# Other distances between the operands of a product in SBUF, one block of products moved ahead in the cross-attention, and four idle products fewer

## The chip, the cores and the metric

The kernel runs on one NeuronCore of a Trainium2 chip. Its time is the device time of one launch in microseconds, taken as the median of several runs. A profile is one execution recorded by the hardware profiler; its times count from the first instruction.

## The reference

One layer of a bidirectional encoder over 512 tokens of 1024 features, in float32. Two mixers (a state-space scan and a gated MLP in chunks) are merged and added to the residual; then comes cross-attention to 256 memory tokens with four heads, then a SwiGLU block. What the change touches is the second half:

```python
def memory_cross_attention(hn, memn, w_q, w_k, w_v, w_o):
    q = (hn @ w_q).reshape(bsz, seq, XATTN_HEADS, XATTN_HEAD_DIM)
    k = (memn @ w_k).reshape(bsz, MEM_LEN, XATTN_HEADS, XATTN_HEAD_DIM)
    v = (memn @ w_v).reshape(bsz, MEM_LEN, XATTN_HEADS, XATTN_HEAD_DIM)
    s = jnp.einsum('blhd,bmhd->bhlm', q, k) * (XATTN_HEAD_DIM ** -0.5)
    p = jax.nn.softmax(s, axis=-1)
    o = jnp.einsum('bhlm,bmhd->blhd', p, v).reshape(bsz, seq, D_MODEL)
    return o @ w_o

def swiglu(hn, w_gate, w_up, w_down):
    return (jax.nn.silu(hn @ w_gate) * (hn @ w_up)) @ w_down

def reference(x, mem, ...):
    ...
    h = h + merged @ w_out[i]
    h = h + memory_cross_attention(rms_norm(h, xattn_norm_g[i]), rms_norm(mem, mem_norm_g), ...)
    h = h + swiglu(rms_norm(h, ffn_norm_g[i]), w_gate[i], w_up[i], w_down[i])
    return rms_norm(h, final_norm_g)
```

## The kernel before

**Products in three parts.** Every float32 operand is split into a rounded half and the rest, `hi` and `lo`: `split` (L85, L86) copies on ScalarE (ACT) into a float32r tile and subtracts on VectorE (DVE). Every product then is three products on TensorE (PE), hi x hi, hi x lo and lo x hi, all added in PSUM (`mm3` at L350, `product` at L1273). A product has a stationary operand of 128 columns, loaded by its own instruction (PEld in the profile, done while the product before it streams), and a moving operand of 256 or 512 columns.

**Weights.** A list, `plan`, holds all blocks of weights in the order of use. `next_w` hands out the next block, starts the loads of those that follow (SP's queue) and splits the ones two ahead into three rotating pairs of tiles, `whi` and `wlo`.

**Which operand moves.** In `feat` and in `product` the weights are stationary and the tokens move; in `tokm` the tokens are stationary and the weights move. The cross-attention's keys use `feat` with the memory's tokens `mn` (products of 256 columns, rows pf<-mn), its values `tokm` with the same tokens (512 columns, rows pt<-whi,mn), the queries `product` with the tokens `hn` (rows qx, qv, qq), and gate and up `product` with the tokens `fn` (rows px, pv, pq; one block of each goes through L350, rows pf<-fn). Queries, gate, up and down are computed by Strassen's scheme with seven products in place of eight, on halves of the tokens and of the features; sums of tokens lie in extra tiles (`hsd`, `hse`, `s1`, `s2`, `s4`).

**Where operands lie.** A tile starts at a fixed byte of each partition. The weights' six tiles start at bytes 30,016 to 50,496, all equal modulo 512; the slot that holds first `xn`, then `hn`, then `fn` starts at 70,976, which is the same modulo 512. The kernel lays the halves of the tokens off that start: `APART = (48, 112)` are floats, so `hi` begins 192 and `lo` 448 bytes (modulo 512) from the weights; both are 192 modulo 256, and this is called the distance below. `hn`, `fn`, the keys' `mn` and the token sums of queries, gate and up all have it. `xn`, `w_out`'s, `w_xo`'s and the down block's operands have distance 0. In the values of the memory, where the weights move, they stand at 64 modulo 256 from the tokens.

**The attention.** For each head `scores` makes the products (rows psc), takes the row maxima (L1236), exponentials on ACT (L1239) and scales the probabilities on DVE (L1243); `turn` transposes them on TensorE (rows ppt) and splits them into `p_hi` and `p_lo`; `values` multiplies by the memory's values (rows po, two of six products a head, each in a PSUM bank) and splits the result into `ot`. `w_xo`, the output product, is a `tokm`: it takes four PSUM banks of the five in the pool (rows pt), and goes through four blocks of weights; block 0 needs the values of head 0, block 1 those of head 1, blocks 2 and 3 those of heads 2 and 3. Its last two blocks are held and done token tile by token tile, and a `hook` is called before them, which makes the values of heads 2 and 3. `later(n, f)` and `tick` put work off by so many slots while the program is written; the framework orders each engine's instructions by priority in the order in which they are written and by its own estimate of when each can start, except where `in_order` pins them.

**The start.** `idles(n)` puts n products of a tile of ones on TensorE, pinned in order: ten at the head (each is two rows in the profile), two more in `first_rows` behind the two products (rows pg) that spread the norm's gain `g_row` over the partitions. `first_rows` then scales the first 128 tokens (L563) with that gain and the factor `r`, transposes them (rows ptr) and goes on to the first block of weights.

Of the kernel before, what the change touches and what calls it, by code (L numbers as in the profile page):

```python
# [20 lines left out]
NT = T // P  # L21
KD = D // P
# [30 lines left out]
def hybrid_layer_kernel(  # L53
# [11 lines left out]
    w_q, w_k, w_v, w_xo = w_q[0], w_k[0], w_v[0], w_xo[0]  # L65
# [11 lines left out]
    def bank(name):  # L77
        return pm.tile([P, 512], F32, tag="mm", name=name)

    def aux(name, shape=(P, 512)):  # L80
        return pa.tile(list(shape), F32, tag="aux", name=name)
# [30 lines left out]
        return hi, lo  # L112


    APART = (48, 112)

    def halves_at(t, k, n, off):

        return tuple(t[:, i * k * n + o:(i + 1) * k * n + o].rearrange("p (k n) -> p k n", k=k)
                     for i, o in enumerate(off))  # L120
# [3 lines left out]
    def sums_place(i, k, n, off=(0, 0)):  # L124
        return halves_at(sums_pool[0].tile([P, 2 * k * n + 128], F32R, tag=f"s{i}", name=f"s{i}", bufs=1), k, n, off)
# [196 lines left out]
    def next_w(*key):  # L322
        i = used_w[0]
        used_w[0] += 1
        assert len(plan[i][0]) == len(key) and plan[i][0][1:] == key[1:] and plan[i][0][0] is key[0]
        for j in range(i, min(i + FAR + 1, len(plan))):
            begin(j, i)
            if j - 1 >= len(tiles) and j - 1 <= i + SPLITS:
                split_w(j - 1)
        for j in range(len(tiles), min(i + SPLITS + 1, len(plan))):  # L330
            split_w(j)
        tile_, tiles[i] = tiles[i], None
        return tile_
# [52 lines left out]

    RATE = 0.8

    def tokm(w, c0, act, nk, evac, ntok=NT, last=2, kpt=2, hook=None, cut=None, t0=0):

        toks = range(t0, t0 + ntok)
        ps = {t: bank(f"pt{t - t0}") for t in toks}
        nw = nk // kpt
        held = []
        full = slice(0, 512)
        for wi in range(nw):
            hi, lo = next_w(w, wi * kpt, kpt, c0, 512)
            held.append((wi, hi, lo))
            if hook is not None and wi == nw - last:
                hook()  # L400
            if wi < nw - last:
                todo, held = held, []
                for t in toks:
                    end = cut is not None and t == ntok - 1 and wi == nw - last - 1
                    tok_block(ps[t], t, todo, act, kpt, full, wi == 0, end)
                    if end:
                        cut(None, ps[t])
                tick(1.3 * ntok)
        for t in toks:
            if cut is not None and t == ntok - 1:  # L410
                for i in range(2):
                    p = aux("pcut", (P, 256))
                    tok_block(p, t, held, act, kpt, slice(256 * i, 256 * i + 256), True, True)
                    cut(i, p)
            else:
                tok_block(ps[t], t, held, act, kpt, full, nw == last, True)
                evac(t, ps[t])
            tick(1.3 * len(held))

    def tok_block(ps, t, ws, act, kpt, cs, first, final):  # L420
        tsl = slice(t * P, (t + 1) * P)
        for i, (wi, hi, lo) in enumerate(ws):
            for k in range(kpt):
                kk = wi * kpt + k
                mm3(ps, (act[0](kk, tsl), act[1](kk, tsl)) if callable(act[0]) else
                    (act[0][:, kk, tsl], act[1][:, kk, tsl]),
                    (hi[:, k, cs], lo[:, k, cs]), first and i == k == 0,
                    final and i == len(ws) - 1 and k == kpt - 1)
# [3 lines left out]
    def later(n, fn):  # L432

        side["later"].append((side["now"] + n, fn))
# [23 lines left out]
    def gain(src, name):  # L458
        t = np_.tile([P, D], F32, tag="gain", name=name, bufs=2)
        nc.sync.dma_start(t, src.partition_broadcast(P))  # L460
        return t
# [60 lines left out]
    def token_slot(name, off=(0, 0)):  # L522

        return halves_at(sp.tile([P, 2 * KD * T + 128], F32R, tag="B", name=name), KD, T, off)
# [8 lines left out]
    def idles(n):  # L533
        for i in range(n):
            in_order(nc.tensor.matmul(idle, ones, ones, start=True, stop=True))

    idles(10)
    warm = np_.tile([P, 1], F32, tag="ms", name="warm", bufs=2)
    nc.scalar.activation(warm, mhalf, AF.Square)

# [577 lines left out]
    for t in range(NT):  # L1118
        nc.sync.dma_start(h[:, t, :], x[t * P:(t + 1) * P, :])
    hn_hi, hn_lo = token_slot("hn", APART)  # L1120

    def mq_tile(name, off):
        return ap_.tile([P, KD * M + 64], F32R, tag="mq", name=name, bufs=2)[:, off:off + KD * M]

    mn_hi, mn_lo = (mq_tile(nm, APART[0]).rearrange("p (k t) -> p k t", k=KD) for nm in ("mn_hi", "mn_lo"))
    g_mem = gain(mem_norm_g, "g_mem")

    def mem_norm(t):
# [8 lines left out]
    for t in range(NM):  # L1137
        later(0.2 + t, lambda t=t: mem_norm(t))
    shift = ap_.tile([P, APART[0]], F32, name="shift")
    nc.gpsimd.memset(shift, 0.0)  # L1140
# [6 lines left out]
    def add_evac(half, layer, fin, fin0=None):  # L1147

        def f(t, ps):
            nc.vector.tensor_tensor(h[:, t, HALF[half]], h[:, t, HALF[half]], ps, ALU.add)  # L1150
            sum_sq(hss[:, layer, t, half:half + 1], h[:, t, HALF[half]])
            if half == 1:
                fin(t, hss[:, layer, t, :])
            elif fin0 is not None:
                fin0(t)
        return f
# [36 lines left out]
    part_at = lambda t, i: t[:, i:i + 1024].rearrange("p (k n) -> p k n", k=4)  # L1193
    hops[6], hops[5] = halves_at(sd, 4, 256, APART), halves_at(se, 4, 256, APART)
    hops[3] = (part_at(sd, 2176 + APART[0]), part_at(se, 2048 + APART[1]))

# [25 lines left out]
    def scores(hd):  # L1222
        q_hi, q_lo = qs.pop(hd)
        scale = XD ** -0.5
        prob = ap_.tile([P, NT, M], F32, tag="prob", name="prob", bufs=1) if hd % 2 == 0 else \
            np_.tile([P, NT, M], F32, tag="gain", name="prob", bufs=2)
        for i in range(2):
            ps = bank("psc").rearrange("p (t m) -> p t m", t=2)
            for tt in range(2):
                t = 2 * i + tt  # L1230
                tsl = slice(t * P, (t + 1) * P)
                for k in range(2):
                    mm3(ps[:, tt, :], (q_hi[:, k, tsl], q_lo[:, k, tsl]),
                        (kt_hi[:, 2 * hd + k, :], kt_lo[:, 2 * hd + k, :]), k == 0, k == 1)
            mx, nm, sm, rs = (ap_.tile([P, 2], F32, tag=k, name=k, bufs=4) for k in ("mx", "nm", "sm", "rs"))
            nc.vector.tensor_reduce(mx, ps, AX.X, ALU.max)  # L1236
            nc.vector.tensor_scalar(nm, mx, -scale, None, ALU.mult)
            for tt in range(2):
                nc.scalar.activation(prob[:, 2 * i + tt, :], ps[:, tt, :], AF.Exp, bias=nm[:, tt:tt + 1],  # L1239
                                     scale=scale, accum_out=sm[:, tt:tt + 1])  # L1240
            nc.vector.reciprocal(rs, sm)
            for tt in range(2):
                nc.vector.tensor_scalar(prob[:, 2 * i + tt, :], prob[:, 2 * i + tt, :], rs[:, tt:tt + 1], None, ALU.mult)  # L1243
        return prob
# [11 lines left out]
    def values(hd, p_hi, p_lo):  # L1256
        for dt_ in range(2):
            ps = bank("po")
            cs = slice(hd * XD + dt_ * P, hd * XD + dt_ * P + P)
            for mt in range(NM):  # L1260
                mm3(ps, (vts[0][:, mt, cs], vts[1][:, mt, cs]), (p_hi[:, mt, :], p_lo[:, mt, :]), mt == 0, mt == NM - 1)
            split(ot_hi[:, 2 * hd + dt_, :], ot_lo[:, 2 * hd + dt_, :], ps)
# [35 lines left out]
    pts = {}  # L1298

    def turn(hd, probs):  # L1300
        pts[hd] = turn_probs(hd, probs)
# [39 lines left out]
    ot_lo = slot("E", (P, KD, T), F32R, "ot_lo")  # L1341
    values(0, *pts.pop(0))
    probs2 = scores(2)
    turn(1, probs1)
    probs3 = scores(3)
    values(1, *pts.pop(1))
    turn(2, probs2)
    later(1, lambda: turn(3, probs3))

    g_f = gain(ffn_norm_g[0], "g_f")  # L1350
    ot = (ot_hi, ot_lo)
    fn_hi, fn_lo = token_slot("fn", APART)
    fn = (fn_hi, fn_lo)

    tokm(w_xo, 0, ot, KD, add_evac(0, 1, None), hook=lambda: [values(i, *pts.pop(i)) for i in (2, 3)])
    at.close()
    ff = ExitStack()
    fp = ff.enter_context(tc.tile_pool(name="ffn", bufs=1))
# [46 lines left out]
    a11, a12, a21, a22 = full[:, K0, T0], full[:, K1, T0], full[:, K0, T1], full[:, K1, T1]  # L1405

    def make_op(q, i, src):
        ops[q] = sums_place(i, 4, 256, APART)
        split(*ops[q], src)

    def sum1():
# [13 lines left out]
    ops = {1: fn_q(K0, T0), 2: fn_q(K1, T0), 7: fn_q(K0, T1), 4: fn_q(K1, T1)}  # L1425
# [86 lines left out]
    for i, u in enumerate(UNITS):  # L1512
        final = i == len(UNITS) - 1
        x, v = begun
        q = unit_bank("pq")
# [122 lines left out]
    for i in range(2):  # L1638
        p = aux("pcut", (P, 256))
# [37 lines left out]
```

## Time and profile before

| what | value |
|---|---|
| median of 3 runs (lowest to highest) | 914.19 us (914.08 to 915.07) |
| the profiled execution | 917.2 us, span of the instructions 915.4 us |
| TensorE products, weight loads | 98% and 87% of the span |
| VectorE, ScalarE, GpSimd | 68%, 52%, 11% |
| DMA | 153.80 MB, mean 168 GB/s |
| keys | about 418 to 443 us |
| values of the memory | about 443 to 466 us |
| queries, scores | about 466 to 519 us |
| probabilities, values, `w_xo` | about 519 to 578 us |
| gate and up | about 578 to 810 us |
| down | from about 792 us to the end |

In rows of groups, "out<-in" names the tile written and those read, then come the operand sizes and the count, and behind the bar the busy time, the mean ns of one and the idle time before. Products overlap in the pipeline, so the ns of one is longer than the step from one to the next. Idle time is put down to the work that ended last.

### The profile page before, as it was taken

Reading aid. Unit: us, or ns where it says so; the run is one execution under the profiler, and the core shown is the slowest. Engines: PE = TensorE matmul, PEld = TensorE weight load, DVE = VectorE, ACT = ScalarE, POOL = GpSimd, SP = SyncE. Lnnn points to the kernel's source line nnn. Section 1 sums busy time; section 2 is a strip of 40 time slices with the busy share of each in tenths; the row PEclk is TensorE's granted clock in tenths of the full one; section 3 lists DMA queues with packets and bytes.
Section 4 is the critical chain, followed back from the end, with each engine's and each line's share of the span. In section 5 each row is a group of like instructions: output and inputs, shape, how many; then the busy total and the mean of one; then the engine's idle time right before and its main releaser. Section 6 shows DMA issues by size and latency. Waiting matters only on the chain.

```text
span 915.4 us, 14510 instructions
## 1 busy us (share of the span) xinstructions
PE 900.7 (98%) x5650; PEld 796.5 (87%) x5650; DVE 623.8 (68%) x1018; ACT 475.4 (52%) x696; POOL 102.1 (11%) x161
## 2 busy tenths in 40 slices
PE   9999999999999999999999999999999999999996
PEld 6888888888888887789899878999999999988885
DVE  5696662888753236858956836776778767899875
ACT  5542985144364334447655634745455454655664
POOL 1004420110025200101000001100020100000000
PEclk9999999999999999999999999999999999999999
DMA  8456574685546577863578416526788873246672
GB/s 252 148 148 185 124 181 141 174 193 149 153 134 146 127 219 206 275 198 120 175 216 252 139 47 184 161 88 149 189 202 212 221 186 93 69 138 200 191 244 90
DMA packets 111974, 153.80 MB, mean 168 GB/s; under 512 B 13521, under 2 KB 78561, under 8 KB 111842
## 3 DMA queue, kind: packets, MB, share of 16 engines
q1 hardware_dynamic: 93026, 128.27, 44.1%
q0 software_dynamic: 16288, 23.57, 15.9%
q10 hardware_dynamic: 2592, 1.05, 0.5%
q8 instruction: 44, 0.72, 0.3%
q14 instruction: 24, 0.20, 0.1%
HBM read 146.08 MB, written 38.24 MB: 201 GB/s over the span
## 4 chain that ended last, share of the span: by engine, by line
PE 90%; ACT 4%; DVE 3%; issue 1%; POOL 0%; DMA 0%; POOLq 0%; SPq 0%; DVEq 0%; ACTq 0%
PE pf L350 27%; PE pt L350 16%; PE px L1273 12%; PE pq L1273 6%; PE dx L350 6%; PE dq L350 3%; PE pv L1273 3%; PE qx L1273 2%; PE dv L350 2%; PE pk L786 2%; PE ptr L506 1%; PE qq L1273 1%; DVE wlo L86 1%; PE po L350 1%; ACT whi L85 1%
## 5 line engine op out<-in xcount | busy, mean ns | idle before, releaser
L86 DVE TENSOR_TENSOR wlo<-wraw,whi 128x1024 fp32r<-128x1024 f32 (+1 forms) x139 | 164.9, 1187 | 109.5 <-ACT whi L85 107.8
L85 ACT CAST whi<-wraw 128x1024 fp32r<-128x1024 f32 (+1 forms) x139 | 142.2, 1024 | 163.0 <-PE pf L350 67.0
L350 PE MATMUL pf<-xn,whi 128*128 128x512 f32 x448 | 140.1, 392 | 0.0
L350 PEld LDWEIGHTS pf<-xn,whi 128*128 128x128 f32 x448 | 83.5, 188 | 17.0 <-issue 0.2
L350 PE MATMUL pf<-xn,wlo 128*128 128x512 f32 x224 | 87.4, 390 | 0.0
L1273 PE MATMUL px<-fn,whi 128*128 128x256 f32 x480 | 86.2, 281 | 0.0
L1273 PEld LDWEIGHTS px<-fn,whi 128*128 128x128 f32 x480 | 73.4, 188 | 0.3 <-ACT u L1532 0.2
L86 DVE TENSOR_TENSOR wlo<-b,whi 128x1024 fp32r<-128x1024 f32 x40 | 48.9, 1222 | 32.8 <-ACT whi L85 32.8
L85 ACT CAST whi<-b 128x1024 fp32r<-128x1024 f32 x40 | 42.0, 1051 | 56.2 <-PE px L1273 28.9
L1273 PE MATMUL px<-fn,wlo 128*128 128x256 f32 x240 | 67.5, 281 | 0.0
L1273 PE MATMUL pq<-s,whi 128*128 128x256 f32 x320 | 57.0, 281 | 0.0
L350 PE MATMUL dx<-whi,s 128*128 128x512 f32 x170 | 53.8, 391 | 1.4 <-ACT whi L85 1.0
L86 DVE TENSOR_TENSOR wlo<-t,whi 128x1024 fp32r<-128x1024 f32 x30 | 36.7, 1224 | 20.9 <-ACT whi L85 20.9
L85 ACT CAST whi<-t 128x1024 fp32r<-128x1024 f32 x30 | 31.5, 1051 | 36.8 <-PE pv L1273 13.3
L350 PEld LDWEIGHTS pf<-xn,wlo 128*128 128x128 f32 x224 | 42.1, 188 | 8.7
L1273 PEld LDWEIGHTS pq<-s,whi 128*128 128x128 f32 x320 | 48.9, 188 | 0.1
L1273 PEld LDWEIGHTS px<-fn,wlo 128*128 128x128 f32 x240 | 46.0, 192 | 0.0
L1273 PE MATMUL pq<-s,wlo 128*128 128x256 f32 x160 | 45.0, 281 | 0.0
L350 PE MATMUL pt<-whi,xn 128*128 128x512 f32 x128 | 42.6, 405 | 0.0
L350 PEld LDWEIGHTS dx<-whi,s 128*128 128x128 f32 x170 | 31.7, 188 | 8.3 <-ACT whi L85 1.2
L350 PE MATMUL dx<-wlo,s 128*128 128x512 f32 x85 | 33.2, 391 | 0.4 <-DVE wlo L86 0.4
L1273 PEld LDWEIGHTS pq<-s,wlo 128*128 128x128 f32 x160 | 30.7, 192 | 0.0
(414 smaller groups left out, 2235.4 us busy)
## 6 DMA issues: line engine op xcount, KB each, us to landing
wraw<-in_w_in_dram SPq DMA_DIRECT2D x36, 512.0 KB, 3.8
dsum<-in_w_down_dram SPq DMA_DIRECT2D x20, 512.0 KB, 6.7
wraw<-dsum SPq DMA_DIRECT2D x20, 512.0 KB, 4.4
b<-in_w_gate_dram SPq DMA_DIRECT2D x15, 512.0 KB, 4.6
b<-in_w_up_dram SPq DMA_DIRECT2D x15, 512.0 KB, 4.6
wraw<-in_w_down_dram SPq DMA_DIRECT2D x15, 512.0 KB, 3.7
dsum<-in_w_down_dram POOLq DMA_DIRECT2D x10, 512.0 KB, 6.8
dsum<-dsum POOLq DMA_DIRECT2D x10, 512.0 KB, 7.4
```

The costliest lines, as they stand in the source:

```text
L85: hi = nc.scalar.copy(dst_hi, src)
L86: lo = nc.vector.tensor_tensor(dst_lo, src, dst_hi.bitcast(F32), ALU.subtract)
L350: nc.tensor.matmul(ps, a[x], b[y], start=start and i == 0, stop=stop and i == 2, skip_group_check=free)
L506: nc.tensor.transpose(ps[:, j, :], src[:, k * P:(k + 1) * P], ident)
L786: nc.tensor.matmul(ps[32 * j:32 * j + 32, q, :], bd[i][:, g].rearrange("p d c -> p (d c)"), lc(es[i], g), start=(i == 0), stop=False, tile ...
L1273: nc.tensor.matmul(ps[:, j, :], a[x], b[y], start=start and j == k == i == 0, stop=k == 3 and i == 2, skip_group_check=True)
```

## The change

Four edits. The distance of `fn` and of the token sums of gate and up becomes 160 and 416 bytes in place of 192 and 448 (`APART_F`), the distance of the memory's tokens `mn` 224 in place of 192 (`APART_K`); the queries' operands stay. In the values of the memory, where `mn` is stationary, the weights then stand 32 modulo 256 from the tokens instead of 64. In the attention, the scores of head 3 are written before the transposes of head 1, and the values of head 1 and the transposes of heads 2 and 3 are no longer written before `w_xo` (and, for head 3, one slot later) but as a hook before its second block, so that its first block comes ahead of them; the values of heads 2 and 3 stay before its third block. At the start, `idles(10)` becomes `idles(6)`.

```diff
+    APART_K = 56
+    APART_F = (40, 104)
...
-    def tokm(w, c0, act, nk, evac, ntok=NT, last=2, kpt=2, hook=None, cut=None, t0=0):
+    def tokm(w, c0, act, nk, evac, ntok=NT, last=2, kpt=2, hooks={}, cut=None, t0=0):
...
-            if hook is not None and wi == nw - last:
-                hook()
+            if wi in hooks:
+                hooks[wi]()
...
-    idles(10)
+    idles(6)
...
-    mn_hi, mn_lo = (mq_tile(nm, APART[0]).rearrange("p (k t) -> p k t", k=KD) for nm in ("mn_hi", "mn_lo"))
+    mn_hi, mn_lo = (mq_tile(nm, APART_K).rearrange("p (k t) -> p k t", k=KD) for nm in ("mn_hi", "mn_lo"))
...
     values(0, *pts.pop(0))
     probs2 = scores(2)
+    probs3 = scores(3)
     turn(1, probs1)
-    probs3 = scores(3)
-    values(1, *pts.pop(1))
-    turn(2, probs2)
-    later(1, lambda: turn(3, probs3))
+
+    def second():
+        values(1, *pts.pop(1))
+        turn(2, probs2)
+        turn(3, probs3)
+
+    def last_two():
+        for i in (2, 3):
+            values(i, *pts.pop(i))
...
-    fn_hi, fn_lo = token_slot("fn", APART)
+    fn_hi, fn_lo = token_slot("fn", APART_F)
...
-    tokm(w_xo, 0, ot, KD, add_evac(0, 1, None), hook=lambda: [values(i, *pts.pop(i)) for i in (2, 3)])
+    tokm(w_xo, 0, ot, KD, add_evac(0, 1, None), hooks={1: second, 2: last_two})
...
-        ops[q] = sums_place(i, 4, 256, APART)
+        ops[q] = sums_place(i, 4, 256, APART_F)
```

## The prediction

> **What bounds the kernel now.** I read the page's busy times and its chain first, then TensorE's groups by shape, then three kinds of stretch: products in steady flow, the start, and the attention outputs.
>
> ```profile
> PE 900.7 (98%) x5650; PEld 796.5 (87%) x5650; DVE 623.8 (68%) x1018; ACT 475.4 (52%) x696; POOL 102.1 (11%) x161
> ...
> PE 90%; ACT 4%; DVE 3%; issue 1%; POOL 0%; DMA 0%; POOLq 0%; SPq 0%; DVEq 0%; ACTq 0%
> ```
>
> TensorE is busy for 98% of the span and 90% of the chain. A change therefore pays if it shortens the step from one product to the next, or if it fills one of the few holes. The groups of TensorE by shape show that equal shapes don't cost the same:
>
> ```profile
> L1273 PE MATMUL px<-fn,whi 128*128 128x256 f32 x480 | 86.2, 281 | 0.0
> L1273 PE MATMUL qx<-hn,whi 128*128 128x256 f32 x96 | 16.6, 276 | 0.0
> L350 PE MATMUL pt<-whi,mg_hi 128*128 128x512 f32 x64 | 24.6, 392 | 0.0
> L350 PE MATMUL pt<-whi,mn_hi 128*128 128x512 f32 x32 | 11.4, 397 | 0.0
> ```
>
> Gate and up (px<-fn) take 281 ns a product, the queries (qx<-hn) 276, though hn and fn are one slot with the same distances. The stretches give the step itself (columns: stretch, its length, then PE busy with the number of products that touch it):
>
> ```profile
> 434.00:442.00 8.00, 8.00 (x70) 8.00 (x69) 7.35 (x8) 6.16 (x8) 0.00 (x0) 1.00 0.45 141
> ...
> 467.00:481.00 14.00, 14.00 (x126) 14.00 (x125) 7.45 (x8) 7.66 (x10) 0.85 (x1) 1.00 0.74 227
> 519.00:522.00 3.00, 1.94 (x12) 1.27 (x11) 2.91 (x12) 3.00 (x12) 0.00 (x0) 1.00 0.27 109
> ...
> 610.00:790.00 180.00, 180.00 (x1531) 180.00 (x1530) 133.94 (x133) 90.42 (x110) 18.35 (x17) 1.00 0.69 170
> ```
>
> About two products hang over the ends of each stretch: 180.00/1529 is 117.7 ns a step in gate and up, 8.00/68 is 117.6 in the keys, 14.00/124 is 112.9 in the queries. Starts in the timeline agree: gate and up 117.7, queries 113.3. The keys had both: 113.3 from 428.40 to 430.78, then, after two groups of transposes, 117.7 to their end, at an unchanged distance. With 512 columns the step is 226.7 at distance 0 (399.78 to 401.14) and 233.3 in the values of the memory (449.63 to 451.96), whose weights stand 64 bytes off the tokens. So there is a toll of 4.4 to 6.6 ns that some streams pay and others don't.
>
> The chain's first pieces (start, us, what) show the second place:
>
> ```profile
> 1.07 4.63 PE idle L535 x20
> 5.70 3.71 PE pg L558 x4
> 9.40 1.17 PE idle L535 x4
> 10.57 0.04 issue
> 10.62 1.13 PE ptr L506 x4
> ```
>
> The idle products lead the chain: ten are 20 rows, 213 ns each. The weight loads in the timeline show the third, where transposes wait for the softmax:
>
> ```profile
> 520.05 0.40 PEld L1252 LDWEIGHTS ppt<-ident,prob 128*128 128x128 f32 x2 [0.56 <-DVE prob L1243]
> 521.37 0.40 PEld L1252 LDWEIGHTS ppt<-ident,prob 128*128 128x128 f32 x2 [0.92 <-DVE prob L1243]
> 521.76 0.30 PEld L350 LDWEIGHTS po<-p_hi,vt 128*128 128x128 f32 x2
> 522.10 0.19 PEld L350 LDWEIGHTS pt<-whi,ot_hi 128*128 128x128 f32 x1
> ```
>
> **The distances, gate and up.** Nothing is added: same products, same order. They are 10 units x 7 x 24 = 1680 on L1273, and 192 on L350 (pf<-fn,s 96, pf<-fn,whi 64, pf<-fn,wlo 32): 1872, all at distance 192 (modulo 256) now and 160 after. No row has distance 160, and no product of 256 or 512 columns streams from a start that is not a multiple of 64 bytes, as these will, so the step is bounded by rows. Below: 113.3, the lowest that any 256-column stream reaches, which is 1872 x 4.4 = 8.2 us less. Above: the 512-column toll of 6.6 ns on top of 113.3 is 119.9, or 1872 x 2.2 = 4.1 us more; products next to transposes reach 124 to 126 ns for one or two steps (431.68 to 431.94), which if it lasted would be 1872 x 7.3 = 13.7 us. I take 113.3: the toll comes and goes at one distance, so it is an interplay of the two reads and not a fixed price of the shape, and moving one of them by 32 bytes disturbs an interplay that now repeats for 230 us. That is a judgement, about even odds.
>
> [...]
>
> **Give-back.** At a 4% shorter step DVE in that stage goes from 133.94/180 = 74% to 77%; ACT and DMA (0.69) have more room. One wait there, 1.02 us at 801.43 (dx on ACT's whi), and the ones near it may grow: +0.5 (0 to +1.5).
>
> **Keys, values of the memory, queries.** Keys: 192 products, about 100 of them with the toll: -0.5 if it goes, +0.5 if it spreads to all. Values: their distance goes from 64 to 32; 96 x 6.6 = -0.6 if the toll goes, else 0; I take 0. The queries (336 products) keep their distance, but start out of another stream; if they take the toll it is 336 x 4.4 = +1.5. I take 0.
>
> **Start.** Four idle products fewer are 8 rows x 213 ns = 1.7 us off the head of the chain. Next late are pg's rows, which need g_row (issued at 0.75; x's first half, issued behind it, was in use at 4.27), then DVE's L563, which needs r. POOL has r at 6.63, from sums that no idle product delays. pg's first half would be done at 6.0 instead of 7.7, ACT's copy (0.59) at 6.6, L563 at 6.75 instead of 8.42: the cover is all but used up, and 1.67 remains. The loads behind it seem to leave room: no wait for a DMA shows between 5 and 27 us. What can eat it is the clock: the first 8 transposes take 0.21 us each, those at 17.39 0.11, so TensorE runs at half pace until about 13.5. If full pace still comes only then, some five products of 512 columns at 427 instead of 233 cost up to 0.9, partly inside DVE's wait at 14.4 to 15.6. I take -1.4, bounds -1.7 and +0.9.
>
> [...]
>
> **w_xo's first block ahead.** Its 24 products need head 0's values alone, whose halves DVE ends by 516.9, and whi and wlo of 510 to 514.5. Now they stand behind turn(2)'s transposes, which wait 0.56 and 0.92 for prob. Ahead of them they give 24 x 0.227 = 5.4 us of work, in which DVE ends the last prob (524.9) and the p halves. So the hole, 1.06 us of PE and 1.5 of PEld, closes. What is late next: head 1's values now come when four of five PSUM banks hold pt, so its second half waits for the split of the first: 0.59 on ACT and 0.69 on DVE. Sixteen transposes of 0.11 = 1.8 us and half of block 1 can stand in there. On DVE and ACT the order of that head's splits and the probs changes, the number doesn't; SP's g_f load (0.5 MB) still waits for turn(1), and its user comes 40 us later. The wait of 0.84 at 538 (head 2's split) stays. I take -1.2; bounds -1.9 (every wait between 519 and 530) and +1.3 (one split fully exposed, hole not closed).
>
> **Sum.** -8.2 + 0.5 - 0.5 + 0 + 0 - 1.4 - 1.2 = -10.8. The profiled execution took 917.2 (span 915.4 and 1.8 around it), 3.0 over the median of the runs, 914.19; the same work is in both: 917.2 - 10.8 = 906.4, and as a median of runs 903.4.
>
> **Rivals.** A difference up to 0.2%, 1.8 us, counts as none: about what a measurement of this kernel can tell.
> 1. *Distances do nothing* (keys flipping at one distance speaks for it, 226.7 against 233.3 against it): only start and hole remain, 914.2 - 2.6 = 911.6; with the clock term lost, 913.
> 2. *A heavier toll in gate and up*, the rival on the slow side: at the new distance the read of the tokens and that of the next weights get in each other's way in all products of a triple, not in part of them. Place: the 1872 products, px, pv and pq rows at 286 ns or more. Price at 121.5, between 118.8 (the last ten pcut rows, 256 columns at distance 0) and 124: 1872 x 3.8 = +7.1, so 914.2 + 7.1 - 2.6 = 918.7. It decides from a step of 117.7 + 2.6/1872 = 119.1; from 120.1 the kernel is slower by over 0.2%. For it: the only other 256-column distance in the trace, pcut's, is slower than gate and up. Against it: those rows are few and mixed with 512-column ones.
> 3. *Half a gain*: one product of each three keeps a toll, step about 115.5: 914.2 - 4.1 - 2.6 = 907.5.
>
> **How the numbers follow.** Forecast (step near 113.3) 0.47, rival 1 0.2, rival 2 0.23, rival 3 0.1. The time is the forecast's, 903.4. Its own range is 902.0 to 906.0, from the bounds of start and hole. The range for 8 in 10 goes from 902.0 through rivals 3 and 1 into rival 2, to a step of 120.8: 911.6 + 1872 x 3.1 = 917.5. It leaves out that rival's dearer half (0.12) and a little below (0.05). Faster by over 0.2%: 0.47 + 0.1 + 0.14 of rival 1 = 0.71, less 0.05 for hole and start both going wrong, 0.66. Within 0.2%: the rest of rival 1 and the mild end of rival 2, 0.10. Slower: 0.24.
>
> **What would show it.** px, pv and pq rows at 276 ns, and some 1588 products in a 180 us stretch of gate and up: right; 281: rival 1; 286 and more: rival 2. Twelve idle rows in place of twenty before pg, L563 at 6.75 and the first transposes at 8.9, with 0.21 us each until when. pt rows directly behind the psc rows, no ppt wait on prob over 0.3 us, and head 1's two po groups apart by less than 2 us of other work. Wrong would also be a wait for DVE or a DMA in gate and up that is longer than now, or queries at 281.

## The result and the profile after

The change makes the kernel slower. First timing: median 919.05 us (917.2 to 919.49, 5 runs), ratio to the kernel before 1.0046, 95% interval 1.0032 to 1.0061. A second timing, again beside the kernel before: 917.25 against 913.95 us, ratio 1.0036 (1.0024 to 1.0049). The profiled execution took 919.36 (span 917.6).

The page's busy times and the chain's shares of the kernel after:

```profile
PE 904.1 (99%) x5642; PEld 799.3 (87%) x5642; DVE 624.2 (68%) x1018; ACT 475.3 (52%) x696; POOL 101.2 (11%) x161
...
PE 89%; ACT 4%; DMA 2%; DVE 2%; issue 1%; SPq 1%; POOL 1%; POOLq 0%; DVEq 0%; ACTq 0%
```

TensorE is busy for 3.4 us more than before, though four idle products (1.7 us) are gone: the same products take longer. Part of that is a window of half clock at the start of this execution (below): the second profile of the same kernel has none, and its PE is busy for 901.4. The groups of TensorE by shape (busy us, mean ns of one) show it in the queries and hide it in gate and up:

```profile
L1277 PE MATMUL px<-fn,whi 128*128 128x256 f32 x480 | 86.7, 281 | 0.0
L1277 PE MATMUL qx<-hn,whi 128*128 128x256 f32 x96 | 17.1, 280 | 0.0
```

px stays at 281 ns in the mean but takes 86.7 us in place of 86.2; qx goes from 276 to 280. The stretches shown of before, in the kernel after (stretch, length, busy time of each engine with the number of instructions that touch it):

```profile
434.00:442.00 8.00, 8.00 (x69) 8.00 (x69) 7.34 (x10) 6.04 (x9) 0.00 (x0) 1.00 0.43 146
467.00:481.00 14.00, 14.00 (x121) 14.00 (x120) 7.42 (x7) 7.17 (x10) 0.66 (x1) 1.00 0.70 227
519.00:522.00 3.00, 3.00 (x23) 2.79 (x23) 3.00 (x12) 2.89 (x13) 0.00 (x0) 1.00 0.00 0
610.00:790.00 180.00, 180.00 (x1520) 180.00 (x1519) 133.10 (x133) 89.65 (x109) 18.38 (x17) 1.00 0.67 170
```

- Gate and up: 180.00/1518 = 118.6 ns a step (117.7 before). The forecast had 1588 products here; there are 1520.
- Queries: 14.00/119 = 117.6 ns in place of 112.9, at an unchanged distance (117.8 and 113.3 by the starts).
- Keys: 69 products in place of 70; over the whole stage the mean step, from the starts of all products in the trace, is 121.0 ns, 119.0 before.
- 519 to 522: PE is full where it had 1.06 us of holes. The order of w_xo does what it was to do.

Between the same instructions of the two profiles, in us: first pf product of the start +0.15, keys +0.37, queries and scores +1.07 (+1.35 up to the third head's scores; the kernel before itself loses 0.27 behind them), from the last psc to the second half of w_xo -1.20, gate and up +1.60, end +2.14. The medians differ by more (3.3 and 4.9), because the profiled execution of before was itself 3.0 over its median; what stood in those 3.0 us is taken up below.

The start, as the timeline shows it:

```profile
1.06 2.93 PE L539 MATMUL idle<-ones 128*128 128x128 f32 x12 [1.06 <-DVE dcol L736]
3.92 3.78 PE L562 MATMUL pg<-g_row,ones 1*128 1x512 f32 x4
7.63 1.22 PE L539 MATMUL idle<-ones 128*128 128x128 f32 x4
8.91 1.97 PE L510 MATMUL ptr<-ident,xt 128*128 128x128 f32 x8
```

Twelve idle rows, and the first transposes at 8.91 (10.62 before), as forecast. The first pf product starts at 44.93 all the same (44.78 before). Two stretches of this profile, and the same two of the second profile of the same kernel, tell why; the third number from the right is the granted clock:

```profile
30.60:34.00 3.40, 3.40 (x23) 2.80 (x23) 2.75 (x12) 1.56 (x2) 0.00 (x0) 1.00 0.00 0
34.10:37.40 3.30, 3.30 (x10) 2.53 (x9) 1.23 (x1) 2.41 (x3) 0.00 (x0) 0.50 0.92 214
```

```profile
30.60:34.00 3.40, 3.40 (x22) 2.86 (x23) 2.75 (x12) 1.63 (x2) 0.00 (x0) 1.00 0.00 0
34.10:37.40 3.30, 3.30 (x16) 2.74 (x15) 1.54 (x3) 2.91 (x5) 0.00 (x0) 1.00 0.84 235
```

In the first, TensorE ran at half clock from 34.03 to 37.44 and did 10 products where the other execution did 16; the other's first pf product starts at 43.17. The 1.7 us of the idle products were there, and one window of half clock, which not every execution has, took them.

Ahead of w_xo, the weight loads after:

```profile
520.63 0.19 PEld L353 LDWEIGHTS pt<-whi,ot_hi 128*128 128x128 f32 x1
...
521.89 0.59 PEld L1256 LDWEIGHTS ppt<-ident,prob 128*128 128x128 f32 x4
...
529.86 0.19 PEld L353 LDWEIGHTS pt<-whi,ot_hi 128*128 128x128 f32 x1 [0.50 <-ACT ot_hi L85]
```

The first w_xo product loads right behind the last psc, the transposes wait for nothing, and the new wait is 0.50 for a split of head 1's values.

### The profile page after: what moved, and what is told of

It is laid out like the page before. It is cut to its first block, busy times and chain, and to the rows that moved or that the text cites. A ratio compares the mean times of both kernels' runs of the same rounds, so it can differ in the third digit from the quotient of the medians.

```text
span 917.6 us, 14495 instructions
## 1 busy us (share of the span) xinstructions
PE 904.1 (99%) x5642; PEld 799.3 (87%) x5642; DVE 624.2 (68%) x1018; ACT 475.3 (52%) x696; POOL 101.2 (11%) x161
## 4 chain that ended last, share of the span: by engine, by line
PE 89%; ACT 4%; DMA 2%; DVE 2%; issue 1%; SPq 1%; POOL 1%; POOLq 0%; DVEq 0%; ACTq 0%
PE pf L353 27%; PE pt L353 16%; PE px L1277 12%; PE pq L1277 6%; PE dx L353 5%; PE dq L353 3%; PE pv L1277 3%; PE qx L1277 2%; PE dv L353 2%; PE pk L790 2%; PE qq L1277 1%; PE psc L353 1%; PE ptr L510 1%; PE po L353 1%; DMA slab<-in_s_log_step_dram 1%
## 5 line engine op out<-in xcount | busy, mean ns | idle before, releaser
L1277 PE MATMUL px<-fn,whi 128*128 128x256 f32 x480 | 86.7, 281 | 0.0
L353 PE MATMUL pt<-whi,xn 128*128 128x512 f32 x128 | 44.6, 421 | 0.3 <-ACT xn L85 0.2
L353 PEld LDWEIGHTS pt<-whi,xn 128*128 128x128 f32 x128 | 25.2, 200 | 6.6 <-ACT xn L85 0.7
```

Of the source, the lines that this page charges most:

```text
L353: nc.tensor.matmul(ps, a[x], b[y], start=start and i == 0, stop=stop and i == 2, skip_group_check=free)
L1277: nc.tensor.matmul(ps[:, j, :], a[x], b[y], start=start and j == k == i == 0, stop=k == 3 and i == 2, skip_group_check=True)
```

## The experiments

The theory after the comparison: the step of a stream of 256 columns is a pace that depends on the distance and on what ran ahead of it; the change put three streams on a worse pace. The rivals were the start, the order, and a mere matter of streams that follow each other. "Ratio" is always against the kernel before, run beside it on the same chip.

### e1_idle6: six idle products alone

```diff
-    idles(10)
+    idles(6)
```

> The kernel before with six idle products at the head instead of ten, nothing else. Theory: the first transposes come 1.7 us earlier (8.9 instead of 10.6), but the 16 small transposes pbc at 31.5 to 33.4 then lie inside one window of the clock, and TensorE runs 3.4 us at half pace behind them, so the first pf row starts at 44.8 +- 0.3 as before and the time is that of before within 0.5 us; queries at 113.3 ns a step, gate and up at 117.7. Rival: the half pace of the changed kernel was chance of that one execution; then the gain of 1.4 us lasts and the time is 912.8.

914.26 us, ratio 0.9995 (0.9986 to 1.0005). The profile had no half-clock window, and its first pf product started at 43.12, 1.66 before that of the kernel before. So the gain is not gone by rule; it was gone in the one execution profiled of after. Nor was the theory's condition met: the changes of the clock in a profile lie whole multiples of 3.413 us apart (in after: 13.55, 34.03, 37.44), and counted on from 11.61, where it opens here, a stretch ends at 32.09, between the 16 small transposes (31.31 to 33.25). The timing can't tell the gain from nothing.

### e2_fn160: gate and up at 160 alone

```diff
+    APART_F = (40, 104)
-    fn_hi, fn_lo = token_slot("fn", APART)
+    fn_hi, fn_lo = token_slot("fn", APART_F)
-        ops[q] = sums_place(i, 4, 256, APART)
+        ops[q] = sums_place(i, 4, 256, APART_F)
```

> The kernel before with gate's and up's tokens at distance 160 instead of 192, nothing else. Theory: the distance itself makes the step of gate and up 118.6 to 119.4 instead of 117.7, which is 1872 x 0.9 to 1.7 = 1.7 to 3.2 us slower, 916 to 917.4. Rival: the step is handed on from the stream ahead and the distance does nothing; then 117.7 and 914.2.

915.83 us, ratio 1.0013 (1.0004 to 1.0022). Its stretch of gate and up:

```profile
610.00:790.00 180.00, 180.00 (x1519) 180.00 (x1519) 132.29 (x131) 90.61 (x110) 18.33 (x17) 1.00 0.67 168
```

1519 products as in the whole change. The starts in the trace repeat 120, 116, 117, 119, 122 ns where before they repeat 118, 117, 118; between the first px and the end of gate and up that is 1.58 us. The move by 32 bytes does it, with nothing else changed. (The weights stay in place in every run, so whether the distance counts or the tokens' own address is not told apart; "distance" stands for both.)

### e3_mn224: the keys' tokens at 224 alone

```diff
+    APART_K = 56
-    mn_hi, mn_lo = (mq_tile(nm, APART[0]) ... for nm in ("mn_hi", "mn_lo"))
+    mn_hi, mn_lo = (mq_tile(nm, APART_K) ... for nm in ("mn_hi", "mn_lo"))
```

> The kernel before with the memory's tokens at distance 224 instead of 192, nothing else. Theory: the keys lose 0.4 us, and the queries, which start behind the values of the memory, take the step of 117.7 instead of 113.3 though their own distance is unchanged: 336 x 4.4 = 1.5 us, in sum 1.9 us slower, 916.1. Rival: the queries' step comes from elsewhere (chance, or the start); then they stay at 113.3 and the time is 914.6.

916.47 us, ratio 1.0021 (1.0011 to 1.0031): as dear as the 1872 products of gate and up, from a stage of 192. The keys go from 119.0 to 121.0 ns in the mean of the stage, and the queries, which this kernel doesn't touch, from 113.4 to 117.1 (117.8 until about 502 us):

```profile
467.00:481.00 14.00, 14.00 (x121) 14.00 (x120) 7.20 (x7) 7.18 (x9) 0.85 (x1) 1.00 0.70 221
504.00:508.00 4.00, 4.00 (x38) 4.00 (x37) 3.13 (x6) 1.45 (x5) 0.00 (x0) 1.00 0.93 256
```

121 products as in the whole change, 126 in the kernels whose memory tokens stand at 192. Behind two groups of transposes at about 502 us the queries run at 113.3 again (by the starts; second row). So the pace of this stream depends on what ran ahead of it. Whether that is the keys or the values, whose weights this edit puts 32 in place of 64 bytes from the tokens, the run doesn't separate.

The keys themselves are six streams of 10 to 93 products (and one of 3) with groups of four transposes between them. By the starts from the sixth product on, at 192 the first five run at 113.2 to 113.5 and the last at 117.8, in all eleven profiles that have this distance; at 224 every one runs at 117.0 to 118.6, behind the same groups, in all five.

### e4_hook: w_xo's first block ahead alone

```diff
-    turn(2, probs2)
-    later(1, lambda: turn(3, probs3))
...
-    tokm(w_xo, ..., hook=lambda: [values(i, *pts.pop(i)) for i in (2, 3)])
+    tokm(w_xo, ..., hooks={1: second, 2: last_two})
```

> The kernel before with w_xo's first block in front of the values of head 1 and the transposes of heads 2 and 3, nothing else. Theory: the hole at 519 to 522 closes and the time is 1.2 us less, 913.0, with queries at 113.3 and gate and up at 117.7. Rival: the moved block changes the step of the products behind it (w_xo, gate and up) and the gain is lost; then 914 to 915 with w_xo's step above 228.

914.43 us, ratio 0.9993 (0.9982 to 1.0005). Its order shows as in the whole change, its worth does not show in the time.

### e5_after and e6_nodist: the whole change, and the same without its distances

```diff
-    APART_K = 56
-    APART_F = (40, 104)
+    APART_K = 48
+    APART_F = (48, 112)
```

> The whole change again, beside the two kernels below. Theory (the four edits add up): their single timings were -0.05%, +0.13%, +0.21% and -0.07%, in sum +0.22%, so a ratio near 1.0022 (some 916.5 to 917 us). Rival (they make each other worse, above all the start, whose half-clock window lies differently each time): 1.0046 as timed before, some 919 us.

> The change without its distances: six idle products and w_xo's first block ahead, all tokens back at 192 bytes. Theory (the distances alone make the change slower): gate and up at 117.8 ns a step, queries at 113.3 from their first product, and a ratio of 0.998 to 1.000 (912.5 to 914.2 us); the whole change is longer by 1.6 + 1.35 + 0.4 = 3.3 us, 0.36%. Rival (the new start or the new order of w_xo loses too): ratio above 1.001, and the whole change only some 2 us above this one.

The whole change: 917.25 us, 1.0036 (1.0024 to 1.0049); the four single edits sum to 1.0022, which lies just below, and each of the four is known to about 0.001 either way. Without the distances: 914.36 us, 1.0001 (0.9992 to 1.0010). So the distances cost 917.25 - 914.36 = 2.9 us, near the 1.6 + 1.35 + 0.4 = 3.3 read from the stages, and the rest of the change is worth nothing that shows, where 2.6 us had been forecast.

### e7_kick: groups of transposes between the streams

```diff
+    def kick(n):
+        p = aux("kick", (P, 4, P))
+        for i in range(n):
+            in_order(nc.tensor.transpose(p[:, i % 4, :], ident, ident))
...
+    kick(4)
     qx, qq_ = unit_bank("qx"), None
...
+    kick(4)
     gate_part(0, T0)
...
     for i, u in enumerate(UNITS):
+        kick((2, 1, 2, 3, 4, 6, 8, 1, 3, 5)[i])
```

> Keys at 224 and values at 32 bytes as in the change, gate and up back at 192; and groups of transposes of the identity, whose result nobody reads, are put between the values of the memory and the queries (4), ahead of gate and up (4), and at the head of each of the ten units (2, 1, 2, 3, 4, 6, 8, 1, 3, 5). 43 of them at 0.11 us are some 4.7 us. Theory (the step is a state that a stream hands on, and an interruption throws it anew): the queries go to another step at the group, 113.3 instead of 117 to 118 until about 502; and the units of gate and up are no longer all alike: at least one of them runs at 113.3, 0.74 us for its 168 products. Rival (the step of a stream belongs to its addresses and shape): all units at 117.8, the queries at 117 to 118 until about 502 as without the group.

(The distance of gate and up is 192, as in e6_nodist.) One run, 916.37 us. Four transposes ahead of the queries set them to 113 from their third product (first row: the queries); the other rows are gate and up behind groups of 1, 2, 3 and 4:

```profile
467.00:481.00 14.00, 14.00 (x126) 14.00 (x125) 7.22 (x7) 7.20 (x9) 0.85 (x1) 1.00 0.67 224
```

```profile
628.00:645.00 17.00, 17.00 (x147) 17.00 (x146) 11.01 (x12) 7.93 (x11) 1.28 (x1) 1.00 0.63 172
648.00:665.00 17.00, 17.00 (x153) 17.00 (x152) 12.86 (x13) 8.79 (x11) 1.45 (x2) 1.00 0.69 177
668.00:684.00 16.00, 16.00 (x143) 16.00 (x143) 10.53 (x12) 7.76 (x10) 3.01 (x3) 1.00 0.78 208
687.00:704.00 17.00, 17.00 (x147) 17.00 (x146) 12.45 (x13) 8.39 (x11) 1.33 (x1) 1.00 0.78 206
```

147 and 153 products in equal time, at one distance, in one kernel: 117.8 and 113.4 ns by the starts. The ten units ran at 117.8, 117.8, 113.4, 113.4, 117.8, 117.8, 117.8, 117.8, 113.4 and 115.5 (the last 113.4 until products of 512 columns come between). Each kept its pace until something other than the stream interrupted it. The rival falls.

### e8_fn128: gate and up at 128

The lines show the difference to e6_nodist.

```diff
-    APART_F = (48, 112)
+    APART_F = (32, 96)
```

> As the change without its distances, but gate and up's tokens 128 bytes from the weights (192 before, 160 in the change). Theory (what counts is whether the tokens start on a multiple of 64 bytes): as at 192, 117.8 ns a step or the 113.3 that streams at 192 also reach, so no loss or 8.3 us less. Rival (the step rises as the tokens come nearer to the weights: 117.8 at 192, 118.65 at 160): 119.5 at 128, 1872 x 1.7 = 3.2 us longer between the first px and the end of gate and up.

One run, 915.57 us:

```profile
610.00:770.00 160.00, 160.00 (x1351) 160.00 (x1350) 117.56 (x117) 79.14 (x96) 18.33 (x17) 1.00 0.75 185
```

That is 118.6 ns, and 1.8 us more than e6_nodist between the first px and the end of gate and up. Neither expectation fits: it is as 160, neither 117.8 nor 119.5. No rule for the distance came out of it.

### e9_mid3, e10_mid5, e11_three: one group in the right place

The line added to e6_nodist (with `kick` as above):

```diff
     unit_second(UNITS[0], begun[1])
+    kick(3)        # e10_mid5: kick(5); e11_three: also ahead of the first two units
     for i in range(2):
         gate_part(i, T1)
```

> The change without its distances, and one group of three transposes of the identity, which nobody reads, in gate and up: behind the second product of the first unit, ahead of the second token half of the last gate block. Theory (an interruption throws the step into one of two states, 113.4 or 117.8, and the products then keep it): either the group leaves 117.8 and costs 0.35 us (ratio 1.0005), or the 1776 products behind it run at 113.4, 1776 x 4.4 = 7.8 us less, 907 us, ratio 0.992. Three transposes led to 113.4 in both units that had them. Rival (a state thrown by a group dies out within a unit or two, as the units with groups could not show): the step is back at 117.8 before 650 us, and the time within 0.1% of the kernel before.

> As with three transposes, but five at the same place: 0.55 us. Theory: one of the two states again, 0.992 or 1.001, and not by need the same as with three. Rival (dies out): within 0.1% of the kernel before.

> Groups of three at the same place and ahead of the first and the second unit's fifth product: 1.05 us. Theory: behind one of the three the step is 113.4 and stays there to the end of gate and up; if behind the last, 1500 x 4.4 = 6.6 us less 1.05, 908.5 us, ratio 0.994. Rival (dies out, or three transposes led there by chance): each stretch may differ, and the time lies between 0.994 and 1.001.

e9_mid3: 914.48 us, 0.9998 (0.9987 to 1.0009); the group of three left 117.8. e10_mid5: 907.45 us, **0.9926** (0.9912 to 0.9940); the group of five led to 113.4, and the step stayed there until products of 512 columns come in at 781 us. e11_three: 908.6 us, 0.9941 (0.9928 to 0.9954); the first group left 117.8, the second led to 113.4, the third kept it. The stretch from 610 to 770, first e9_mid3, then e10_mid5:

```profile
610.00:770.00 160.00, 160.00 (x1361) 160.00 (x1360) 118.75 (x119) 80.21 (x97) 18.33 (x17) 1.00 0.77 187
```

```profile
610.00:770.00 160.00, 160.00 (x1414) 160.00 (x1413) 121.09 (x120) 84.03 (x102) 18.35 (x17) 1.00 0.77 187
```

160.00/1412 = 113.3: the forecast's step of gate and up, reached at 192 bytes and not by another distance. DVE and ACT fit the 4% more products into the same time.

"Dies out" falls: the pace held for 193 us. All 11 runs of e9_mid3 lie between 912.3 and 916.1 us and all 6 of e10_mid5 between 906.0 and 909.3, so by the times a program comes to the same pace each time. Which group leads where is not settled: three transposes gave both. Nor is it settled whether the transposes themselves do it or the half microsecond by which they put off the products behind them; no run has the delay without them.

### e12_kick160: the groups of e7_kick in the whole change

The lines show the difference to e7_kick.

```diff
-    APART_F = (48, 112)
+    APART_F = (40, 104)
```

> The whole change with the groups of transposes of the kernel that had them in every unit (4 ahead of the queries and of gate and up, then 2, 1, 2, 3, 4, 6, 8, 1, 3, 5), gate and up at 160 as in the change. Theory (the slow state's pattern belongs to the distance, the fast state to any distance): some units at 113.4, the others at 118.65. Rival (at 160 bytes there is no fast state): all ten units at 118.5 to 118.8.

One run, 920.29 us. The ten units ran at 120.0, 118.7, 118.65, 117.35, 117.3, 117.3, 118.7, 118.7, 118.7 and 119.2 ns (means of starts in the trace). The first and the fifth of them:

```profile
609.00:626.00 17.00, 17.00 (x144) 17.00 (x144) 11.72 (x13) 8.44 (x11) 2.21 (x2) 1.00 0.78 205
689.00:706.00 17.00, 17.00 (x147) 17.00 (x147) 12.30 (x14) 7.91 (x11) 1.33 (x1) 1.00 0.78 197
```

So 160 has at least three paces, thrown anew by the same groups, but 113.4 came up behind none of the eleven groups; at 192 it came behind four of eleven. The rival was nearer: no fast pace at 160 was found, though not one pace either. The queries, again behind four transposes, went to 113.3 as in e7_kick.

### e13_only5 and e14_idle2: what the other edits are worth

```diff
     unit_second(UNITS[0], begun[1])
+    kick(5)
```

```diff
-    idles(10)
+    idles(2)
```

> The kernel before with the group of five transposes in gate and up alone: ten idle products, old order of w_xo, all tokens at 192 bytes. Theory (the group alone leads gate and up to 113.4; idle products and order are worth about nothing): ratio 0.9915 to 0.9935, as with them. Rival 1 (the other edits do give 1 to 2.6 us, hidden by noise): 0.994 to 0.996. Rival 2 (what a group does hangs on the whole history of the program): 117.8 and 1.0006.

> The kernel before with two idle products in place of ten at the head: 16 rows at 213 ns, 3.4 us off the head of TensorE's chain. Theory (the start goes by when the clock opens, about 11.3 to 14.1 us in the profiles so far, and only in some executions by a window before that, which more idle products make likelier): no early window, the first pf at 42.5 to 43.5 us as with six, and a ratio of 0.9985 to 1.0005. Rival (the head of the chain counts): the first pf at 40 to 41.5, ratio 0.9955 to 0.997.

The kernel before with the group of five alone: 907.28 us, **0.9917** (0.9902 to 0.9932), as good as with six idle products and the new order, with 1415 products from 610 to 770 us. It is the simplest version that beats both kernels.

Two idle products: 913.75 us, 0.9989 (0.9980 to 0.9998). The expected range just holds it, but the first pf product came at 42.05, 0.45 before what the theory said, so the theory that only the clock counts is too strong: the head of the chain counts for part. That rests on one profile, whose clock also opened earliest of all, at 10.80.

e13_only5 also gives a second profile with ten idle products and the old order. Its first pf product stands at 44.75, within 0.03 of before's. But the hole ahead of w_xo is shorter (weight loads):

```profile
518.75 0.68 PEld L1252 LDWEIGHTS ppt<-ident,prob 128*128 128x128 f32 x6
520.25 0.40 PEld L1252 LDWEIGHTS ppt<-ident,prob 128*128 128x128 f32 x2 [0.82 <-DVE prob L1243]
```

One wait of 0.82 where before's profile had 0.56 and 0.92. ACT's rows some 15 us ahead show the cause, first in the kernel before, then here:

```profile
504.06 1.05 ACT L85 CAST whi<-wraw 128x1024 fp32r<-128x1024 f32 x1 [1.79 <-DMA wraw<-in_w_xo_dram]
...
508.34 0.48 ACT L1239 ACTIVATE prob<-psc,nm 128x256 f32<-128x256 f32 x1 [2.25 <-DVE nm L1237]
```

```profile
502.18 1.05 ACT L85 CAST whi<-wraw 128x1024 fp32r<-128x1024 f32 x1
...
506.76 0.48 ACT L1239 ACTIVATE prob<-psc,nm 128x256 f32<-128x256 f32 x1 [2.55 <-DVE nm L1237]
```

In the profiled execution of before a load of w_xo's weights came late, ACT waited 1.79 for it with the softmax queued behind, and its next prob started 1.6 later. None of the other fifteen profiles has that wait for w_xo. From the last psc to the second half of w_xo before took 35.5 us, e13_only5 34.5, and the kernels with the new order 34.3.

## Why the prediction was wrong

The forecast, 903.4 us with 902.0 to 917.5, was on the wrong side; 919.05 lies above the range, the second timing's 917.25 just inside its upper edge (which by its own sum, 911.6 + 5.8, is 917.4).

1. **Distances, gate and up: -8.2 taken, +1.6 measured.** The failed step is "moving one of them by 32 bytes disturbs an interplay that now repeats". That the toll is no fixed price of the shape was right, and so were 113.3 as the fast pace and the bounds (113.3 to 119.9; it is 118.65); that it is an interplay of the two reads no run shows. Wrong was what ends it: the move by 32 bytes (e2_fn160) gave 118.65. The trace held the answer: the keys flipped, from 113.3 to 117.7, at an unchanged distance behind two groups of transposes. An interruption can move a stream to another pace (from 117.8 to 113.4 in e10_mid5); which paces came up differed with the distance, and at 160 (eleven groups, 117.3 to 120.0) and 224 (the keys, 117.0 to 118.6) none was fast.
2. **Rival 2 was right in place and direction, too high in price.** The step is 118.65 where it took 121.5, below its own point of decision, 119.1. That point held 2.6 us of gains elsewhere, which did not come. Its mechanism, a toll in all three products of a triple, is not shown: the steps at 160 repeat in fives. Its sign, px rows at 286 ns or more, did not come: they stayed at 281, which the prediction gives to rival 1. The mean ns of a row hid a change of 0.9 in the step; the count of products in the stretch showed it.
3. **Queries: 0 taken, +1.35 measured.** The text named the case ("if they take the toll it is +1.5") and gave it nothing, though it had seen the keys change pace at one distance; its sign for this, queries at 281 ns, came (280). **Keys: -0.5 taken, +0.4 measured**, the named other end. Values: 0, right (233.4 and 233.2 ns in the mean of the stage).
4. **Give-back: +0.5 taken, next to none found.** In e13_only5, where the step did fall to 113.3, gate and up took 6.98 us less from the first px to the end. The products at the fast pace behind the group are 1728 (two of the last three groups of 24 stay at 117.8), and 1728 x 4.4 - 0.55 is 7.1. The time, 7.6 us less (0.0083 x 914.8) with an interval of 1.4 either way, is too coarse to tell.
5. **Start: -1.4 taken.** Between profiles with neither an early window of full clock nor one of half clock it is the full 1.7: first pf at 43.1 (43.06 to 43.17 in e1_idle6, e5_after, e7_kick, e8_fn128 and e11_three) against 44.75 and 44.78; e11_three and e13_only5 (43.09 and 44.75) also have the clock opening at the same 14.10. But executions differ by as much: over all profiles the mean is 43.3 with six idle products (ten profiles) and 44.1 with ten (five), 0.8 less, and the timing of e1_idle6 says 0.5 less, with an interval down to 1.3 less and up to 0.5 more. Part of it: a first, early window of full clock (before 12 us) stands in three of the five profiles with ten idle products and in three of the ten with six. That the idle products buy this window was not tried by itself. The clock that lasts opens anywhere from 10.80 (e14_idle2) to 14.10 us (e11_three, e13_only5), and the windows before it are 3.41 us long.
6. **Hole: -1.2 taken, and -1.2 between the two profiles, but 0.2 to 0.3 against an execution without the late load.** The order did what the step said; but the transposes' wait that it was to fill was 0.82 of weight loading in the other execution in place of 1.48, and the new order has a wait of its own, 0.50.
7. **From profile to median.** The prediction saw that the profiled execution was 3.0 over the median and said "the same work is in both". It was not: the late load was in the profile alone (1.3 us against e13_only5: 0.27 in the last scores, 1.0 behind them), and its start, 44.78, stood at the slow end of the spread, whose mean is 44.1. The sum took 2.6 us out of the median that were, for a good part, the profile's own surplus.

By rival 1, that distances do nothing, e2_fn160 and e3_mn224 would be at 1.0; they are at 1.0013 (1.0004 to 1.0022) and 1.0021 (1.0011 to 1.0031). What it had for it holds too: a step of 113.4 or 117.8 at one address (e7_kick, e10_mid5) depends on what ran before. What in the chip makes the paces is not shown by any run.

## What to carry to other kernels

When streams of equal products run at different steps, look for where the step changes within one stream, and what stands there: here, at one set of addresses, a handful of transposes decided between 113.4 and 117.8 ns, and five of them (0.55 us) were worth 7.5 us. An edit ahead of a long stream can change its pace without touching it (e3_mn224: the queries from 113.4 to 117.1 ns), so read the step of every stage after any change. And when the profiled execution is longer than the median, look first for what it has that the others need not have (here a late transfer, 1.3 us, and in the kernel after a window of half clock, 1.8 us), and take no gain from there.

## What the hardware showed that was not expected

- Paces of one stream of 256 columns, float32r: 113.4 or 117.8 ns at 192 bytes (e7_kick); 117.35, 118.7 or 120.0 at 160 (e12_kick160); about 118.6 at 128 (e8_fn128). A pace lasted for some 1,700 products over 193 us in e10_mid5. It changed only where transposes or products of 512 columns came between, and not behind all of these (e9_mid3: 117.8 on both sides of three transposes); by the times, the same program found the same one each time (11 runs of e9_mid3 at 912.3 to 916.1 us, 6 of e10_mid5 at 906.0 to 909.3).
- TensorE's clock fell to one half in the middle of a busy kernel: for 3.41 us from 34.03 in the kernel after, right behind 16 transposes of 32 columns (31.51 to 33.45). Four of the sixteen profiles have such a window between 32 and 37.5 us; it cost the kernel after 1.8 us (first pf at 44.93 against 43.17 in the second profile of the same kernel). In each profile the changes of the clock lie whole multiples of 3.413 us apart. Counted that way, 1.75 to 1.94 us of the 16 transposes fell into the one stretch of 3.413 us ahead of the window in those four (after, e3_mn224, e4_hook, e9_mid3), and at most 1.69 into any one stretch in eleven of the other twelve. The twelfth, e11_three, had all 1.94 in one and kept its clock, so that is not the whole condition. Which executions have it was not brought under control.
